# Small numbers of a fused encoder block in one tile, and where the matmuls' operands then start

## The chip, the core and the metric

The kernel runs on one core of a Trainium2 chip. A core has TensorE (PE; its weight loads are shown apart as PEld), VectorE (DVE), ScalarE (ACT), GpSimd (POOL) and SyncE (SP), which here issues the transfers. The metric is the time of one execution in device microseconds, the median of three runs. SBUF has 128 partitions; where a tile "starts" is the byte within each partition.

## The reference

One layer of an encoder block on 256 tokens of 2048 channels, all in float32:

```
u = rmsnorm(h) * g_mix;  proj = u @ w_in                 # 2048 x 4096
y_f = per group of 256 channels: Re(DFT2 over positions x channels) @ w_f[g]   # 4 groups
y_a = attention, 8 heads of 128, three dilated windows merged, ALiBi distances
h = h + concat(y_f, y_a) @ w_out                         # 2048 x 2048
u = rmsnorm(h) * g_mlp
h = h + square(relu(u @ w_up)) @ w_down                  # 2048 x 8192, 8192 x 2048
out = rmsnorm(h) * g_fin
```

## The kernel before

Every large product is made of three: a number is split into hi (as float32r, 12 significant bits) and lo (the rest), and hi*hi + hi*lo + lo*hi are added up in PSUM. Activations are split once into tiles that stay in SBUF (u, y_hi, y_lo). Weights are stored in the order of their use, in chunks of 128 partitions by 2048 numbers (1 MB). `load_next` brings a chunk into a w_raw buffer and splits it, in two halves, into w_hi (ACT, L112) and w_lo (DVE, L113); each of the three has three buffers, and two chunks are loaded ahead.

Two loops use the chunks:
- `strip` (matmuls of `mm3`, L120 to L122; the first chunk's at L197): the activations are stationary, the weights move. One strip is 4 chunks x 2 token tiles x 4 rows of tiles x 3 products = 96 matmuls of 512 columns.
- `column` (L220, L221): one chunk holds 128 columns of weights, which are stationary; the activations move. One column is 16 pairs: w_hi times u_hi and u_lo side by side (512 columns), then w_lo times u_hi (256 columns).

In time: two strips of w_in for the Fourier group, with the transforms' small products between them; twice a strip for v and eight columns for q and k, with the heads' attention between the groups; four strips of w_out; then four MLP groups, each of 16 columns (w_up) and four strips (w_down). Groups 0 and 2 keep their hidden activations in y tiles of the pool mlp, groups 1 and 3 in y tiles of the pool acts, which were the Fourier and attention groups' outputs before. The last strip is cut into parts (`products`), the last 72 matmuls having 256 columns, and the last norm (`ending`) follows.

The order of work on an engine is the order in which the program is written; small steps are put between the products by generators (`later`, `part`). Pools lay their tiles one behind the other, and each tile starts at a multiple of 32 bytes. The pool const holds ident and ones (512 bytes each) and root, one number a partition; wpool comes behind it, then acts, then four, att and mlp by turns in the same place. The norms' numbers (`inverse`, `sums`, `ending`) are tiles of acts of one to eight numbers a partition.

Of the kernel before, what the change touches and what calls it, by code (L numbers as in the profile page):

```python
# [16 lines left out]
P = 128  # L17
# [15 lines left out]
FIRST = (4, 4, 2, 2, 2)  # L33
WARM = 9


def _order():
    """The weights by chunks of 128 rows by 2048 numbers, in the order of their use.

    "rows": four row tiles by 512 columns, the moving operand; "cols": 16 row tiles by 128 columns,  # L40
    the stationary operand."""
    todo = []

    def rows(name, row0, col0):
        todo.extend((name, row0 + c * CK * P, CK, col0, NS) for c in range(NN))

    def cols(name, col0):
        todo.append((name, 0, KT, col0, P))

    rows("w_in", 0, 0)  # L50
    rows("w_in", 0, NS)
    for a in range(2):
        rows("w_in", 0, 3 * FOURIER + a * NS)
        for hd in range(a * 4, a * 4 + 4):
            cols("w_in", FOURIER + hd * HD)
            cols("w_in", 2 * FOURIER + hd * HD)
    for n in range(NN):
        rows("w_out", 0, n * NS)
    for gi in range(NGRP):
        for j in range(KT):  # L60
            cols("w_up", gi * D + j * P)
        for n in range(NN):
            rows("w_down", gi * D, n * NS)
    return todo
# [3 lines left out]
def tile_block(ctx: ExitStack, tc: tile.TileContext, gx_t, x, w_all, w_f, g_fin,  # L68
# [27 lines left out]
    nc.vector.memset(ones, 1.0)  # L96
    root = const.tile([P, 1], F32, name="root")
    nc.scalar.activation(root, ones[:, :1], AF.Sqrt)
# [3 lines left out]

    NG = 2 * KT
    gh = acts.tile([P, NG + NM * D], F32, name="gh")
    g_cols = gh[:, :NG]
# [3 lines left out]
    def split(hi, lo, src, scale=None):  # L109
        """hi + lo = src * scale, each in the 12 significant bits that one pass carries."""  # L110
        if scale is None:
            nc.scalar.copy(out=hi, in_=src)  # L112
            nc.vector.tensor_tensor(out=lo, in0=src, in1=f32(hi), op=ALU.subtract)  # L113
        else:
            nc.scalar.activation(hi, src, AF.Copy, scale=scale)
            nc.vector.scalar_tensor_tensor(out=lo, in0=src, scalar=scale, in1=f32(hi),
                                           op0=ALU.mult, op1=ALU.subtract)
# [5 lines left out]

# [1 line left out]
    def hidden_input():  # L125
        u = acts.tile([P, KT, 2 * S], F32R, name="u")
        return u, u[:, :, :S], u[:, :, S:]

    u, u_hi, u_lo = hidden_input()
    order = _order()  # L130
# [41 lines left out]
    def later(gen):  # L172
        """Work that a result asks for: its first part now, each further one after a group of the products that follow."""
        next(gen, None)
        queue.append(gen)
# [10 lines left out]
    def strip(l_hi, l_lo, need=None):  # L186
        """The activations (stationary) times 2048 rows by 512 columns of the weights, for both token tiles."""
        ps = [acc() for _ in range(NM)]
# [22 lines left out]
    def column(r, parts=(KT // 2 - 1, KT - 1), need=None):  # L211
        """128 columns of the weights (stationary), transposed, times the activations.

        The halves of the result, whose sum is asked for: the large products, and the small ones."""
        ps = acc()
        hi, lo = chunk()
        for kt in range(KT):
            if kt == need:
                finish()
            nc.tensor.matmul(ps, hi[:, kt, :], r[:, kt, :], start=kt == 0, stop=False)  # L220
            nc.tensor.matmul(ps[:, S:], lo[:, kt, :], r[:, kt, :S], start=False, stop=kt == KT - 1)  # L221
            if kt in parts:
                part()
        return ps[:, :S], ps[:, S:]
# [7 lines left out]
    def inverse(ss, name):  # L232
        """1 / sqrt(mean of squares + eps), from the sums of squares."""
        n = ss.shape[1]
        a = acts.tile([P, n], F32, name=f"{name}_a")
        nc.vector.tensor_scalar(out=a, in0=ss, scalar1=1.0 / D, scalar2=EPS, op0=ALU.mult, op1=ALU.add)
        r = acts.tile([P, n], F32, name=f"{name}_r")
        nc.scalar.activation(r, a, AF.Sqrt)
        y = acts.tile([P, n], F32, name=f"{name}_y")
        nc.vector.reciprocal(out=y, in_=r)  # L240
        t = acts.tile([P, n], F32, name=f"{name}_t")
        nc.vector.tensor_mul(out=t, in0=y, in1=y)
        nc.vector.tensor_mul(out=t, in0=t, in1=a)
        nc.vector.tensor_scalar(out=t, in0=t, scalar1=-0.5, scalar2=1.5, op0=ALU.mult, op1=ALU.add)
        inv = acts.tile([P, n], F32, name=f"{name}_inv")
        nc.vector.tensor_mul(out=inv, in0=y, in1=t)
        return inv

    def across(inv, room):
        """The tokens' numbers along the free axis, the same on all partitions (in PSUM)."""  # L250
        ps = aux()[:, :S]
        for m in range(NM):
            b = room()
            nc.vector.tensor_scalar_mul(out=b, in0=ones, scalar1=inv[:, m:m + 1])
            nc.tensor.transpose(ps[:, m * P:(m + 1) * P], b, ident)
        return ps

    y_hi = acts.tile([P, KT, S], F32R, name="y_hi")
    y_lo = acts.tile([P, KT, S], F32R, name="y_lo")

# [1 line left out]
    four_ctx = ExitStack()  # L262
# [23 lines left out]

    # cos(a + b) = cos a cos b - sin a sin b, on the even and odd parts along the channels.
    # The packed channels of group gl of two: 128 even ones, then 128 odd ones; the even channel 128,
    # apart, takes the place 32 * gl among the odd ones, and the odd one there the place 0.

    def fold_map(g):
        """The group's linear map after the transform along the channels."""
        wf_hi = four.tile([P, 2, GD], F32R, name="wf_hi")
# [12 lines left out]
    def symmetric(st, ps):  # L306
        """Even and odd parts along the channels."""
        e_hi = four.tile([P, NM, WU], F32R, name="e_hi")
# [25 lines left out]
    def positions(g):  # L334
        """The transform along the positions."""
        st, gl = divmod(g, 2)
# [23 lines left out]

# [1 line left out]
    inv_q = acts.tile([P, S], F32, name="inv_q")  # L362
    inv_k = acts.tile([P, S], F32, name="inv_k")
    inv1 = []
# [28 lines left out]

# [1 line left out]
    later(timeline({6: [(add_squares, 0), (add_squares, 4)]}))  # L395
# [19 lines left out]

# [1 line left out]
    att_ctx = ExitStack()  # L417
# [11 lines left out]
    def channels(ps, name, inv):  # L429
        """One head of q or k, with the head's channels on the partitions."""  # L430
        t = total(ps, att)
# [52 lines left out]

# [1 line left out]
    u2, u2_hi, u2_lo = hidden_input()  # L486
    junk = att.tile([P, NS], F32, name="junk")

# [3 lines left out]
    def sums(ss, name):  # L492
        t = acts.tile([P, ss.shape[1]], F32, name=f"{name}_s")
        nc.vector.tensor_reduce(out=t, in_=ss, op=ALU.add, axis=AX.X)
        return t

    ss2 = acts.tile([P, NM, NN], F32, name="ss2")

# [26 lines left out]

# [1 line left out]
    inv_u = acts.tile([P, S], F32, name="inv_k")  # L527
# [7 lines left out]

    ss3 = acts.tile([P, NM, NN], F32, name="ss3")
    for gi in range(NGRP):
# [22 lines left out]

# [1 line left out]
    NH2 = NS // 2  # L562
    tail = [[(acc(), slice(0, NS))], [(aux()[:, :NH2], slice(0, NH2)), (aux()[:, :NH2], slice(NH2, NS))]]
    base = acts.tile([P, NM], F32, name="base")
    got = []
# [14 lines left out]

    def small(name):
        return acts.tile([P, 1], F32, name=name)

    def ending(m):
        a = base[:, m:m + 1]
        for i, (ps, cols) in enumerate(tail[m]):
            hs = h[m][:, D - NS + cols.start:D - NS + cols.stop]
            nc.vector.tensor_add(out=hs, in0=hs, in1=ps)
            b = small(f"a{m}{i}")
            nc.vector.tensor_tensor_reduce(out=junk[:, cols], in0=hs, in1=hs, scale=1.0 / D, scalar=a,  # L590
                                           op0=ALU.mult, op1=ALU.add, accum_out=b)
            a = b
        r, y, t, inv = (small(f"{n}{m}") for n in ("r", "y", "t", "i"))
        nc.scalar.activation(r, a, AF.Sqrt)
# [54 lines left out]
def _tiles(weights):  # L649
    """All weights in one array, a chunk after the other, each with its partitions' numbers in a row."""  # L650
    todo = _order()
# [32 lines left out]
```

## Time and profile before

| | |
|---|---|
| time, median of 3 runs | 1036.84 us (1036.69 to 1037.19) |
| profiled execution, first to last instruction | 1035.5 us |
| time of that execution beyond its span | not recorded; the median lies 1.3 us above the span |
| PE, DVE, ACT busy | 99%, 59%, 49% of the span |
| transfers' share of 16 engines | 53.5% |
| matmuls of 512 columns | 3536 |
| matmuls of 256 columns | 1628 |

How to read it: a matmul's own time in the trace is longer than the distance to the next one, since matmuls overlap; its end is modelled. The starts of two neighbours show the rate. In "acc<-u,w_hi" the first operand moves and the second is stationary.

### The profile page before, as it was taken

The numbers are of one execution on the slowest core, as the hardware profiler recorded it, in microseconds if no ns is written. First come the engines' busy times: TensorE is split into PE (matmuls) and PEld (weight loads), VectorE is DVE, ScalarE is ACT, GpSimd is POOL, SyncE is SP. The second block draws the span as 40 slices with busy tenths as digits, with TensorE's granted clock in tenths as the row PEclk, the third lists the DMA queues.
The fourth block names the chain that finished last, engine by engine and source line by source line (L and its number), as shares of the span: only waits on it lengthen the run. The fifth ranks groups of instructions, "written<-read, shape, count | busy, mean of one in ns | idle before, by whom it ended". The sixth has DMA issues, their size and how long they took to land.

```text
span 1035.5 us, 12994 instructions
## 1 busy us (share of the span) xinstructions
PE 1026.0 (99%) x5254; PEld 870.2 (84%) x5254; DVE 610.2 (59%) x846; ACT 502.4 (49%) x741; POOL 1.3 (0%) x10
## 2 busy tenths in 40 slices
PE   9999999999999999999999999999999999999997
PEld 7888888888888888888888888888888888888886
DVE  6875775775456656545656545456555446565553
ACT  7754554554446554333555533345543335554441
POOL 0000000000000000000000000000000000000000
PEclk9999999999999999999999999999999999999999
DMA  9653755444555555555555555555555555555532
GB/s 320 229 223 112 265 170 189 164 170 163 187 220 172 194 191 180 198 202 177 191 194 174 201 186 180 203 172 194 192 180 197 202 178 189 192 177 200 183 142 82
DMA packets 32683, 195.10 MB, mean 188 GB/s; under 512 B 3568, under 2 KB 6128, under 8 KB 10608
## 3 DMA queue, kind: packets, MB, share of 16 engines
q1 hardware_dynamic: 32624, 194.28, 53.5%
q8 instruction: 41, 0.67, 0.2%
q14 instruction: 18, 0.15, 0.0%
HBM read 192.17 MB, written 2.10 MB: 188 GB/s over the span
## 4 chain that ended last, share of the span: by engine, by line
PE 97%; DMA 1%; SPq 0%; DVE 0%; ACT 0%; issue 0%; ACTq 0%
PE acc L220 29%; PE acc L122 16%; PE acc L120 16%; PE acc L121 16%; PE acc L221 15%; PE aux L122 1%; PE aux L120 1%; PE aux L121 1%; DMA w_raw<-w_all 1%; SPq L91 0%; PE aux L509 0%; PE aux L464 0%; DVE w_lo L113 0%; ACT w_hi L112 0%; ACT gh L607 0%
## 5 line engine op out<-in xcount | busy, mean ns | idle before, releaser
L113 DVE TENSOR_TENSOR w_lo<-w_raw,w_hi 128x1024 fp32r<-128x1024 f32 (+1 forms) x356 | 423.8, 1209 | 286.5 <-ACT w_hi L112 286.2
L112 ACT CAST w_hi<-w_raw 128x1024 fp32r<-128x1024 f32 (+1 forms) x356 | 361.8, 1040 | 319.4 <-PE acc L122 230.5
L220 PE MATMUL acc<-u,w_hi 128*128 128x512 f32 x1280 | 450.9, 394 | 0.0
L221 PE MATMUL acc<-u,w_lo 128*128 128x256 f32 x1280 | 362.0, 283 | 0.0
L220 PEld LDWEIGHTS acc<-u,w_hi 128*128 128x128 f32 x1280 | 240.4, 188 | 54.7
L120 PE MATMUL acc<-w_hi,y_hi 128*128 128x512 f32 x624 | 246.7, 395 | 0.0
L122 PE MATMUL acc<-w_hi,y_lo 128*128 128x512 f32 x624 | 245.6, 394 | 0.0
L121 PE MATMUL acc<-w_lo,y_hi 128*128 128x512 f32 x624 | 244.5, 392 | 0.0
L221 PEld LDWEIGHTS acc<-u,w_lo 128*128 128x128 f32 x1280 | 240.7, 188 | 0.2
L122 PEld LDWEIGHTS acc<-w_hi,y_lo 128*128 128x128 f32 x624 | 117.3, 188 | 27.5
L121 PEld LDWEIGHTS acc<-w_lo,y_hi 128*128 128x128 f32 x624 | 117.4, 188 | 26.3
L120 PEld LDWEIGHTS acc<-w_hi,y_hi 128*128 128x128 f32 x624 | 117.4, 188 | 25.4
L533 ACT ACTIVATE sq<-relu 128x256 f32<-128x256 f32 x64 | 26.8, 419 | 118.7 <-DVE relu L531 118.7
L113 DVE TENSOR_TENSOR y_lo<-sq,y_hi 128x256 fp32r<-128x256 f32 x64 | 27.2, 425 | 58.1 <-ACT y_hi L112 58.1
L121 PE MATMUL acc<-w_lo,u 128*128 128x512 f32 x120 | 47.6, 397 | 0.5 <-DVE w_lo L113 0.5
L122 PE MATMUL acc<-w_hi,u 128*128 128x512 f32 x120 | 47.4, 395 | 0.0
L120 PE MATMUL acc<-w_hi,u 128*128 128x512 f32 x120 | 46.9, 398 | 0.1
L229 DVE TENSOR_TENSOR total<-acc,total 128x256 f32<-128x256 f32 x80 | 33.5, 418 | 2.7 <-ACT total L228 2.6
L228 ACT COPY total<-acc 128x256 f32<-128x256 f32 x80 | 29.2, 366 | 8.1 <-PE acc L221 8.1
L556 DVE TENSOR_TENSOR gh<-gh,acc 128x512 f32<-128x512 f32 x30 | 20.5, 684 | 17.9 <-PE acc L122 17.8
L121 PEld LDWEIGHTS acc<-w_lo,u 128*128 128x128 f32 x120 | 22.6, 188 | 5.9 <-DVE w_lo L113 1.4
L112 ACT CAST y_hi<-sq 128x256 fp32r<-128x256 f32 x64 | 26.0, 406 | 2.0
(142 smaller groups left out, 472.5 us busy)
## 6 DMA issues: line engine op xcount, KB each, us to landing
w_raw<-w_all SPq DMA_DIRECT2D x171, 1024.0 KB, 4.7
w_raw<-w_all SPq DMA_DIRECT2D x6, 512.0 KB, 7.7
w_raw<-w_all SPq DMA_DIRECT2D x8, 256.0 KB, 5.0
gh<-x SPq DMA_DIRECT2D x8, 256.0 KB, 7.0
out<-gh SPq DMA_DIRECT2D x6, 256.0 KB, 2.4
gh<-gx_t SPq DMA_DIRECT2D x4, 256.0 KB, 6.3
wf<-w_f SPq DMA_DIRECT2D x4, 256.0 KB, 4.9
g_b<-g_fin SPq DMA_DIRECT2D x1, 1024.0 KB, 4.7
```

Source lines behind the costliest of these rows:

```text
L112: nc.scalar.copy(out=hi, in_=src)
L113: nc.vector.tensor_tensor(out=lo, in0=src, in1=f32(hi), op=ALU.subtract)
L120: nc.tensor.matmul(ps, l_hi, r_hi, start=first, stop=False)
L121: nc.tensor.matmul(ps, l_hi, r_lo, start=False, stop=False)
L122: nc.tensor.matmul(ps, l_lo, r_hi, start=False, stop=last)
L220: nc.tensor.matmul(ps, hi[:, kt, :], r[:, kt, :], start=kt == 0, stop=False)
L221: nc.tensor.matmul(ps[:, S:], lo[:, kt, :], r[:, kt, :S], start=False, stop=kt == KT - 1)
L228: nc.scalar.copy(out=t, in_=ps[1])
L229: nc.vector.tensor_tensor(out=t, in0=ps[0], in1=t, op=ALU.add)
L533: nc.scalar.activation(q, r, AF.Square)
L556: nc.vector.tensor_add(out=hs, in0=hs, in1=ps[m])
```

## The change

A tile few of 224 numbers a partition (896 bytes) joins the pool const, and a function `small` hands out slices of it one behind the other. The norms' numbers, ss2, ss3, base and those of `ending` become such slices. The pool acts is filled in another order: u, y_hi, y_lo, inv_q and inv_k come ahead of gh (which holds 32 gains and then the residual h). Comments and docstrings go; no instruction is added, removed or moved on any engine, and none has another wait. Core of the diff:

```
-    root = const.tile([P, 1], F32, name="root")
+    few = const.tile([P, FEW], F32, name="few")          # FEW = 224
+    few_at = [0]
+    def small(n, *shape):
+        at = few_at[0]
+        few_at[0] += n
+        assert few_at[0] <= FEW
+        t = few[:, at:at + n]
+        return t.rearrange("p (a b) -> p a b", b=shape[0]) if shape else t
+    root = small(1)
...
     NG = 2 * KT
+    u0 = acts.tile([P, KT, 2 * S], F32R, name="u")
+    y_hi = acts.tile([P, KT, S], F32R, name="y_hi")
+    y_lo = acts.tile([P, KT, S], F32R, name="y_lo")
+    inv_q = acts.tile([P, S], F32, name="inv_q")
+    inv_k = acts.tile([P, S], F32, name="inv_k")
     gh = acts.tile([P, NG + NM * D], F32, name="gh")
...
-        a = acts.tile([P, n], F32, name=f"{name}_a")
+        a = small(n)
...
-    ss2 = acts.tile([P, NM, NN], F32, name="ss2")
+    ss2 = small(NM * NN, NN)
...
-    base = acts.tile([P, NM], F32, name="base")
+    base = small(NM)
...
-        r, y, t, inv = (small(f"{n}{m}") for n in ("r", "y", "t", "i"))
+        r, y, t, inv = (small(1) for _ in range(4))
```

Where the tiles start, by the addresses in the two programs (byte in the partition, with its rest by 64 and by 2048):

| tile | before | after |
|---|---|---|
| ident, ones | 16512, 17024 (0; 128, 640) | the same |
| first w_raw; each further w_raw, w_hi, w_lo buffer 8192 on | 17568 (32; 1184) | 18432 (0; 0) |
| u | 107808 (32; 1312) | 92160 (0; 0) |
| y_hi, y_lo of acts | 140576, 156960 (32; 1312) | 124928, 141312 (0; 0) |
| y_hi, y_lo of mlp | 186464, 202848 (32; 96) | 186496, 202880 (0; 128) |
| h in gh | 91424 (32; 1312) | 159872 (0; 128) |
| tables, maps, q, k, v, p of four and att | all (32; several) | all (0; several) |

All slices that a matmul takes of these tiles start at multiples of 512 bytes from the tile's start.

## Rows read from the trace of the kernel before

**Rows 1.** The page, part 1: span, busy time of each engine.
```profile
span 1035.5 us, 12994 instructions
PE 1026.0 (99%) x5254; PEld 870.2 (84%) x5254; DVE 610.2 (59%) x846; ACT 502.4 (49%) x741; POOL 1.3 (0%) x10
```

**Rows 2.** Waits of PE: us in total, times, longest.
```profile
PE aux L101 <- DVE ones L96: 1.1, 1, 1.1
PE acc L121 <- DVE w_lo L113: 0.5, 1, 0.5
```

**Rows 3.** The page, part 4: the chain that ended last, by engine.
```profile
PE 97%; DMA 1%; SPq 0%; DVE 0%; ACT 0%; issue 0%; ACTq 0%
```

**Rows 4.** The page, part 2: granted TensorE clock in 40 slices.
```profile
PEclk9999999999999999999999999999999999999999
```

**Rows 5.** Groups by line and shape, PE and PEld: count | busy us, mean ns.
```profile
L220 PE MATMUL acc<-u,w_hi 128*128 128x512 f32 x1280 | 450.9, 394 | 0.0
L221 PE MATMUL acc<-u,w_lo 128*128 128x256 f32 x1280 | 362.0, 283 | 0.0
L120 PE MATMUL acc<-w_hi,y_hi 128*128 128x512 f32 x624 | 246.7, 395 | 0.0
...
L120 PE MATMUL acc<-w_hi,u 128*128 128x512 f32 x120 | 46.9, 398 | 0.1
L122 PE MATMUL aux<-w_hi,y_lo 128*128 128x256 f32 x32 | 9.0, 282 | 0.0
...
L464 PE MATMUL aux<-ident,s 128*128 128x128 f32 x32 | 4.8, 272 | 0.0
...
L120 PE MATMUL aux<-wf_hi,tab_hi 128*128 128x256 f32 x16 | 4.7, 292 | 0.0
...
L220 PEld LDWEIGHTS acc<-u,w_hi 128*128 128x128 f32 x1280 | 240.4, 188 | 54.7
```

**Rows 6.** Timeline of PE at four stage boundaries: start us, us, instruction.
```profile
403.47 0.39 PE L120 MATMUL acc<-w_hi,y_hi 128*128 128x512 f32 x1
...
491.37 0.40 PE L220 MATMUL acc<-u,w_hi 128*128 128x512 f32 x1
...
581.25 0.40 PE L120 MATMUL acc<-w_hi,y_hi 128*128 128x512 f32 x1
...
670.47 0.40 PE L220 MATMUL acc<-u,w_hi 128*128 128x512 f32 x1
```

**Rows 7.** Timeline of PE, the first and last of the closing 256-column matmuls.
```profile
1019.12 0.28 PE L120 MATMUL aux<-w_hi,y_hi 128*128 128x256 f32 x1
...
1027.55 0.28 PE L122 MATMUL aux<-w_hi,y_lo 128*128 128x256 f32 x1
```

**Rows 8.** Timeline of PE, four transposes in one head.
```profile
119.46 0.60 PE L464 MATMUL aux<-ident,s 128*128 128x128 f32 x4
```

**Rows 9.** Timeline behind the last matmul, two of the small instructions.
```profile
1029.29 0.22 DVE L596 SCALAR_TENSOR_TENSOR t<-y,a 128x1 f32<-128x1 f32 x1
1029.54 0.15 DVE L597 TENSOR_SCALAR t<-t 128x1 f32<-128x1 f32 x1
```

**Rows 10.** Two windows: length, busy us (x) of PE, PEld, DVE, ACT, POOL; clock; transfers.
```profile
5.25:18.71 13.46, 12.77 (x50) 9.02 (x51) 10.17 (x19) 10.22 (x20) 0.00 (x0) 1.00 0.99 333
18.71:1027.83 1009.12, 1009.12 (x5186) 857.31 (x5186) 596.46 (x816) 487.94 (x715) 0.58 (x4) 1.00 0.53 187
```

**Rows 11.** The chain in order of time, 4 to 20 us: start, us.
```profile
10.85 5.47 DMA w_raw<-w_all
...
18.71 0.51 PE acc L121
```

**Rows 12.** Waits of ACT for PE: us in total, times, longest.
```profile
ACT w_hi L112 <- PE acc L122: 230.5, 73, 4.5
...
ACT w_hi L112 <- PE acc L220: 71.3, 74, 3.5
```

**Rows 13.** The page, part 6: transfers of whole chunks, median us to landing.
```profile
w_raw<-w_all SPq DMA_DIRECT2D x171, 1024.0 KB, 4.7
```

**Rows 14.** Timeline of PE in group 1's strips: the longest distance there.
```profile
641.20 0.40 PE L120 MATMUL acc<-w_hi,y_hi 128*128 128x512 f32 x1
641.44 0.40 PE L121 MATMUL acc<-w_lo,y_hi 128*128 128x512 f32 x1
```

More of the change, by code (lines that the diff above doesn't have):

```diff
@@ L34 @@
 WARM = 9
+FEW = 224
 def _order():
@@ L122, in mm3, with hidden_input @@
         nc.tensor.matmul(ps, l_lo, r_hi, start=False, stop=last)
-    def hidden_input():
-        u = acts.tile([P, KT, 2 * S], F32R, name="u")
+    def hidden_input(u):
         return u, u[:, :, :S], u[:, :, S:]
-    u, u_hi, u_lo = hidden_input()
+    u, u_hi, u_lo = hidden_input(u0)
     order = _order()
@@ L234, in inverse @@
         n = ss.shape[1]
-        a = acts.tile([P, n], F32, name=f"{name}_a")
+        a = small(n)
         nc.vector.tensor_scalar(out=a, in0=ss, scalar1=1.0 / D, scalar2=EPS, op0=ALU.mult, op1=ALU.add)
-        r = acts.tile([P, n], F32, name=f"{name}_r")
+        r = small(n)
         nc.scalar.activation(r, a, AF.Sqrt)
-        y = acts.tile([P, n], F32, name=f"{name}_y")
+        y = small(n)
         nc.vector.reciprocal(out=y, in_=r)
-        t = acts.tile([P, n], F32, name=f"{name}_t")
+        t = small(n)
         nc.vector.tensor_mul(out=t, in0=y, in1=y)
@@ L244, in inverse @@
         nc.vector.tensor_scalar(out=t, in0=t, scalar1=-0.5, scalar2=1.5, op0=ALU.mult, op1=ALU.add)
-        inv = acts.tile([P, n], F32, name=f"{name}_inv")
+        inv = small(n)
         nc.vector.tensor_mul(out=inv, in0=y, in1=t)
@@ L256, in across @@
         return ps
-    y_hi = acts.tile([P, KT, S], F32R, name="y_hi")
-    y_lo = acts.tile([P, KT, S], F32R, name="y_lo")
     four_ctx = ExitStack()
@@ L359, in mapped @@
         split(y_hi[:, 2 * g:2 * g + 2, :], y_lo[:, 2 * g:2 * g + 2, :], py)
-    inv_q = acts.tile([P, S], F32, name="inv_q")
-    inv_k = acts.tile([P, S], F32, name="inv_k")
     inv1 = []
@@ L483, in tile_block @@
             later(head(hd, q, k, v, (2, 3, 2) if hd < NH - 1 else (2, 3, 1)))
-    u2, u2_hi, u2_lo = hidden_input()
+    u2, u2_hi, u2_lo = hidden_input(acts.tile([P, KT, 2 * S], F32R, name="u"))
     junk = att.tile([P, NS], F32, name="junk")
@@ L492, in sums @@
     def sums(ss, name):
-        t = acts.tile([P, ss.shape[1]], F32, name=f"{name}_s")
+        t = small(ss.shape[1])
         nc.vector.tensor_reduce(out=t, in_=ss, op=ALU.add, axis=AX.X)
         return t
-    ss2 = acts.tile([P, NM, NN], F32, name="ss2")
+    ss2 = small(NM * NN, NN)
     def residual(ps, n):
@@ L534, in up @@
         split(hidden[0][:, j, :], hidden[1][:, j, :], q)
-    ss3 = acts.tile([P, NM, NN], F32, name="ss3")
+    ss3 = small(NM * NN, NN)
     for gi in range(NGRP):
@@ L579, in products @@
                 kt == 0, kt == KT - 1)
-    def small(name):
-        return acts.tile([P, 1], F32, name=name)
     def ending(m):
@@ L588, in ending @@
             nc.vector.tensor_add(out=hs, in0=hs, in1=ps)
-            b = small(f"a{m}{i}")
+            b = small(1)
             nc.vector.tensor_tensor_reduce(out=junk[:, cols], in0=hs, in1=hs, scale=1.0 / D, scalar=a,
```

## The prediction

> **What bounds the kernel now.** I read the share of each engine first, then who TensorE waits for, then the chain of work that ended last. TensorE (PE) has a matmul in flight for 1026.0 of 1035.5 us, VectorE (DVE) works 59% and ScalarE (ACT) 49% [rows 1]. PE's own waits come to 1.6 us in two places [rows 2], and the chain is 97% PE [rows 3]. So the time is the number of matmuls times the distance between the starts of two neighbours, and the change can move the time by much only if it moves that distance. No other engine and no transfer need be faster for it.
>
> "Busy" does not say that PE runs at its peak. The granted clock is 9 (full) in every slice [rows 4], that is 2.4 GHz, so 512 columns should stream in 512 / 2.4 = 213.3 ns and 256 in 106.7 ns. The mean of one matmul (394 ns, 283 ns) [rows 5] overlaps with the next and is no price; the distance of starts is. It comes out of stage boundaries, since the code gives the number of matmuls between them [rows 6]:
> - strips of MLP group 0 (403.47 to 491.37 us, 4 strips of 96 matmuls of 512 columns): 87.90 us / 384 = 228.9 ns
> - strips of group 1 (581.25 to 670.47): 89.22 / 384 = 232.3 ns
> - columns of group 1 (491.37 to 581.25, 16 columns of 16 pairs, 512 + 256): 89.88 / 256 = 351.1 ns a pair, where 320.0 would do
> - the 72 last matmuls of 256 columns (1019.12 to 1027.55, 71 distances) [rows 7]: 118.7 ns.
>
> A fixed cost per matmul can be had from the transposes: four take 0.60 us together [rows 8], the last alone 0.272 [rows 5], so they start 0.109 us apart. That reads as 256 steps at 2.4 GHz (106.7 ns) and 2.6 ns over. Their moving operand is ident; with ones it is the only operand of a matmul that starts at a multiple of 64 bytes before the change. Every other one, the stationary ones of the transposes included, starts 32 bytes past one.
>
> Taking 2.6 ns off, the excess over streaming is 13.0 ns in group 0's strips: 31 steps in 512 columns, about one in 16 columns, which are 64 bytes of a partition. I call this term A: 13.3 ns for 512 columns, 6.7 for 256. With A out, 3.1 ns (7 steps) are left in group 1's strips, 2.7 in the last matmuls of 256 columns, and 25.9 - 20.0 = 5.9 for two in the columns; next to none in group 0's strips. This is term B, some 3 ns a matmul. Group 0 and group 1 run the same lines on the same weights' buffers and differ in where the stationary tile lies (pool mlp, 96 past a multiple of 2048; pool acts, 1312 past). So one part of the distance does hang on where operands lie.
>
> **The change part by part.** Both programs hold the same instructions in the same order on every engine, with the same waits; only tile names and addresses differ.
>
> *The shared tile.* The square root, the inverses and the last norm's numbers become slices of few. Nothing is added or removed. On the path that sets the end stand only those behind the last matmul, seven or so instructions of 0.15 to 0.22 us [rows 9]. If a slice 4 bytes past the last one made each a tenth faster or slower, that would be under 0.2 us; I take 0, since these instructions read one or two numbers either way.
>
> *The products' operands.* All large tiles move from 32 bytes past a multiple of 64 to a multiple of 64; w_raw, w_hi, w_lo, u and the y of pool acts to a multiple of 2048, the y of pool mlp to 128 past one. I take term A for the price of starting in the middle of 64 bytes and take it away: one step in 16 columns is what each 64 bytes, read in two halves, would cost, and the aligned moving operand of the transposes shows no A. The trace has no matmul of 32-bit numbers at full column rate on an aligned moving operand, so the term is bounded and not read: from below by 0 (the distance stays), from above by all the excess over 2.6 ns.
> Counts [rows 5]: 512 columns 1280 + 3 x 624 + 3 x 120 = 3512 (the three lines of mm3 have one count each; the 24 first ones are left out); 256 columns 1280 + 3 x 32 + 15 x 16 = 1616. Before 18.71 us, 50 matmuls stand [rows 10] behind the first transfers and splits, and the chain there is not PE's [rows 11]; 26 of them are among the 3512 and gain nothing. Sum: 3486 x 13.33 = 46.5 us, 1616 x 6.67 = 10.8 us, together 57.3 us.
>
> *What is late next.* Nothing, by these rows. ACT's splits of weights wait 230.5 + 71.3 us for PE [rows 12], so they come earlier when PE does. From 18.71 us on DVE works 596 and ACT 488 of 1009 us [rows 10]; on a span shorter by 57 us that is 63% and 51%. A chunk of weights takes PE 24 x 232.3 ns = 5.6 us now and 5.3 us then, against 4.7 us to land with three buffers [rows 13]. Where DVE is busiest, at the start (10.2 of 13.5 us in the first stretch of the same group), this cover is thinnest; were it gone there, a few us of the gain would go.
>
> *Sum.* The profiled span is 1035.5 us, the median of the runs 1036.84, so 1.3 us lie around the span. 1035.5 - 57.3 + 1.3 = 979.5, say 980 us. If B went too, everything would run at its columns and 2.6 ns: 768 x 13.0 (groups 0 and 2) + 1280 x 25.9 (pairs) + 1438 x 16.4 + 336 x 9.4 ns = 10.0 + 33.2 + 23.6 + 3.2 = 70.0 us, and 967. The forecast's own range is 965 to 990.
>
> The Trainium skill, page "TensorE: Matmul & The Clock Gate", section Back-to-back issue gap, gives N / 2.4 + 2.5 ns for an isolated warm matmul, 215.8 for 512 columns. The distances above differ from it by 13 to 17 ns, the transposes agree with its 2.5 by 2.6; where it held everywhere the estimate would be the 967 just worked out from rows.
>
> **The rivals.**
> *No change: the excess belongs to reading four bytes a column.* The transposes have half the rate of columns, so they may have room to hide what A is. Then A stays, B at most shifts a little, and the time stays 1036.8. For it: A is the same in places with quite different addresses mod 2048. Against it: the difference of groups 0 and 1 shows that place matters.
> The Trainium skill, page "SBUF — State Buffer", section Specifications, has lines of 16 bytes, and a penalty where an access crosses to a new one. 32 past a multiple of 64 starts such a line as well as 0 does, so by it this change is worth nothing and the time is 1036.8. The trace speaks for 64 and not 16 bytes, with one step in 16 columns, but it does not show the cause.
>
> *Half: only the ends of an operand cost.* 2048 bytes that start in the middle touch 33 blocks of 64 for 32, 1024 bytes 17 for 16. One block of 16 columns is 6.7 ns a matmul, whatever its columns: (3486 + 1616) x 6.67 = 34.0 us, so 1003. Against it: the excess grows with the columns, from 9.4 to 16.4 ns.
>
> *Slower: the two operands collide more.* Stationary and moving operand are read at the same time, a weight load of 188 ns [rows 5] within each 229 or 232. Now they lie 128 (group 1) or 64 bytes (group 0) apart modulo 512. After it, weights, u and y all start at the same place modulo 2048, and group 0's pair has the 128 of group 1 now. If B is such a collision, group 0 and 2's 768 matmuls take group 1's distance, 3.4 ns more: 2.6 us, 1039.4. If equal starts are the worst place, each 512 takes what the worst in the steady strips takes today, 0.24 us [rows 14]: 768 x 11.1 + 2744 x 7.7 = 29.6 us, 1066. It decides from the point where B's growth is above what A gives back, that is with A untouched and the strips over 0.232. For it: B exists and hangs on place. Against it: B is only a fifth of A.
>
> **How the numbers follow.** Forecast (A goes) 0.48, 980; half 0.18, 1003; no change 0.14, 1036.8; slower 0.20, 1039 to 1066. The likeliest is 980. A range from 962 to 1040 holds the first three and the lowest part of the fourth, some 8 in 10. Faster by over 0.2% (2.1 us, about what a measurement of this kernel can tell from no change): 0.48 + 0.18 = 0.66; within: 0.14; slower: 0.20.
>
> **What would show it.** Right: starts in the strips 0.216 to 0.219 us apart and 0.325 to 0.331 a pair in the columns; the transposes still 0.109, weight loads still about 188 ns, PE still 97% of the chain, instructions of DVE and ACT as long as before. Half: 0.222 to 0.226. No change: 0.229 and 0.232 in the same stages. Slower: group 0's strips at or over group 1's. What would make it wrong with A gone: waits of PE for w_hi or w_lo of more than a few us in total, at the start above all.

## The result, and the profile after

The changed kernel takes 1031.67 us (median of 5 runs, 1031.38 to 1032.38) against 1036.84 us before: a ratio of 0.9948, 95% interval 0.9936 to 0.9961. It is faster, by 5.2 us. The forecast was 980 us: the direction was right, the size was wrong by a factor of eleven, and the time lies inside the range only because the range reached to the other cases.

The page of the changed kernel, parts 1 and 4:

```profile
span 1030.6 us, 12994 instructions
PE 1021.0 (99%) x5254; PEld 868.8 (84%) x5254; DVE 609.7 (59%) x846; ACT 502.7 (49%) x741; POOL 1.3 (0%) x10
...
PE 97%; DMA 1%; SPq 0%; DVE 0%; ACT 0%; issue 0%; ACTq 0%
```

Against [rows 1, 3] PE's time fell by 5.0 us and the span by 4.9, weight loads by 1.4, and DVE and ACT changed by at most 0.5: the gain is in the matmuls, as the prediction argued it must be. Its timeline at the stage boundaries, as in [rows 6] (start us, us, instruction; here from the last boundary ahead of w_out's strips on):

```profile
216.71 0.40 PE L138 MATMUL acc<-w_hi,y_hi 128*128 128x512 f32 x1
...
309.91 0.39 PE L237 MATMUL acc<-u,w_hi 128*128 128x512 f32 x1
...
399.88 0.39 PE L138 MATMUL acc<-w_hi,y_hi 128*128 128x512 f32 x1
...
489.11 0.39 PE L237 MATMUL acc<-u,w_hi 128*128 128x512 f32 x1
...
579.55 0.40 PE L138 MATMUL acc<-w_hi,y_hi 128*128 128x512 f32 x1
...
666.62 0.39 PE L237 MATMUL acc<-u,w_hi 128*128 128x512 f32 x1
...
757.06 0.39 PE L138 MATMUL acc<-w_hi,y_hi 128*128 128x512 f32 x1
...
846.30 0.39 PE L237 MATMUL acc<-u,w_hi 128*128 128x512 f32 x1
...
935.05 0.39 PE L138 MATMUL acc<-w_hi,y_hi 128*128 128x512 f32 x1
```

The boundaries before that [rows 6] leaves out:

```profile
217.44 0.39 PE L120 MATMUL acc<-w_hi,y_hi 128*128 128x512 f32 x1
...
312.51 0.40 PE L220 MATMUL acc<-u,w_hi 128*128 128x512 f32 x1
...
760.34 0.40 PE L120 MATMUL acc<-w_hi,y_hi 128*128 128x512 f32 x1
...
848.25 0.40 PE L220 MATMUL acc<-u,w_hi 128*128 128x512 f32 x1
...
938.14 0.40 PE L120 MATMUL acc<-w_hi,y_hi 128*128 128x512 f32 x1
```

Differences of these starts give the length of each stage. Strips have 384 matmuls, columns 256 pairs:

| stage | before, us | after, us | ns a matmul or pair, before | after |
|---|---|---|---|---|
| strips of w_out | 95.07 | 93.20 | | |
| columns, group 0 | 90.96 | 89.97 | | |
| strips, group 0 | 87.90 | 89.23 | 228.9 | 232.4 |
| columns, group 1 | 89.88 | 90.44 | 351.1 | 353.3 |
| strips, group 1 | 89.22 | 87.07 | 232.3 | 226.7 |
| columns, group 2 | 89.87 | 90.44 | 351.1 | 353.3 |
| strips, group 2 | 87.91 | 89.24 | 228.9 | 232.4 |
| columns, group 3 | 89.89 | 88.75 | 351.1 | 346.7 |

(The w_out stage and the columns of group 0 hold the transposes and a wait for the second norm too.) The strips of w_out and of group 1 got faster, and so did those of w_in and of group 3, which the table leaves out; the strips of groups 0 and 2 got slower and took the very pace that group 1 had before. The columns split into a faster pace (346.7) and a slower one (353.3). No stage came near 216 to 219 ns. The transposes' row shows that their distance stayed, at (0.60 - 0.272) / 3 = 0.109 us as in [rows 8]:

```profile
118.87 0.60 PE L476 MATMUL aux<-ident,s 128*128 128x128 f32 x4
```

The 72 last matmuls of 256 columns run from 1014.15 to 1022.67 us, 8.52 / 71 = 120.0 ns; [rows 7] gave 118.7, so these got slower.

### The profile page after: what moved, and what is told of

Same layout as the page of the kernel before. It is cut to its first block, busy times and chain, and to the rows that moved or that the text cites. A ratio compares the mean times of both kernels' runs of the same rounds, so it can differ in the third digit from the quotient of the medians.

```text
span 1030.6 us, 12994 instructions
## 1 busy us (share of the span) xinstructions
PE 1021.0 (99%) x5254; PEld 868.8 (84%) x5254; DVE 609.7 (59%) x846; ACT 502.7 (49%) x741; POOL 1.3 (0%) x10
## 4 chain that ended last, share of the span: by engine, by line
PE 97%; DMA 1%; SPq 0%; DVE 0%; ACT 0%; issue 0%; ACTq 0%
PE acc L237 29%; PE acc L139 16%; PE acc L140 16%; PE acc L138 16%; PE acc L238 15%; PE aux L138 1%; PE aux L140 1%; PE aux L139 1%; DMA w_raw<-w_all 1%; SPq L92 0%; PE aux L521 0%; PE aux L476 0%; DVE w_lo L131 0%; ACT w_hi L130 0%; ACT gh L616 0%
## 5 line engine op out<-in xcount | busy, mean ns | idle before, releaser
L543 DVE SCALAR_TENSOR_TENSOR relu<-total,inv_k 128x256 f32<-128x256 f32 x64 | 26.8, 419 | 0.0
```

The source lines that it names most:

```text
L543: nc.vector.scalar_tensor_tensor(out=r, in0=total(ps, mlp), scalar=0.0, in1=inv_u, op0=ALU.max, op1=ALU.mult)
```

## The experiments

The theories at the start: (1) the distance of starts hangs on the place of the stationary operand relative to the moving one, and the rest by 64 is nothing; (2) a start in the middle of 64 bytes costs, as the prediction had it; (3) what is over 213.3 ns is the weight load beside the matmul, or the four bytes a column.

**Everything 32 bytes further (shift_32).**

```
-FEW = 224
+FEW = 232
```

> The changed kernel with the shared tile 32 bytes longer, so that every large tile starts 32 bytes past a multiple of 64 and all places relative to each other stay. Theory 1 (relative place): as the changed kernel, 1031.7 us, strips of groups 1 and 3 at 226.7 ns, of groups 0 and 2 at 232.4. Theory 2 (the rest by 64): the gain is lost, 1036.8 us or more.

It took 1031.77 us (ratio 0.9953, 0.9941 to 0.9966): nothing of the gain is lost. Its timeline at the boundaries of groups 0 and 1:

```profile
399.19 0.39 PE L138 MATMUL acc<-w_hi,y_hi 128*128 128x512 f32 x1
...
488.42 0.39 PE L237 MATMUL acc<-u,w_hi 128*128 128x512 f32 x1
...
578.86 0.40 PE L138 MATMUL acc<-w_hi,y_hi 128*128 128x512 f32 x1
...
665.93 0.39 PE L237 MATMUL acc<-u,w_hi 128*128 128x512 f32 x1
```

89.23, 90.44 and 87.07 us: each stage as long as in the changed kernel. Theory 2 is out.

**The old order of tiles on the new start (old_order).**

```
+    gh = acts.tile([P, NG + NM * D], F32, name="gh")
     u0 = acts.tile([P, KT, 2 * S], F32R, name="u")
...
     inv_k = acts.tile([P, S], F32, name="inv_k")
-    gh = acts.tile([P, NG + NM * D], F32, name="gh")
```

> The changed kernel with gh ahead of u and y again, as before the change: all large tiles stay at multiples of 64 bytes, but u and all y lie 128 bytes past the weights modulo 512. Theory 1 (relative place): every strip at 232.4 ns, so before's time plus 768 x 3.4 ns = 1039.4 us, slower than before. Theory 2 (the rest by 64): no slower than the changed kernel, 1031.7 us.

It took 1039.44 us, slower than before (ratio 1.0026, 1.0016 to 1.0035), though every large tile starts at a multiple of 64 bytes. The strips of groups 0 and 1:

```profile
403.53 0.40 PE L138 MATMUL acc<-w_hi,y_hi 128*128 128x512 f32 x1
...
492.75 0.40 PE L237 MATMUL acc<-u,w_hi 128*128 128x512 f32 x1
...
582.63 0.40 PE L138 MATMUL acc<-w_hi,y_hi 128*128 128x512 f32 x1
...
671.85 0.40 PE L237 MATMUL acc<-u,w_hi 128*128 128x512 f32 x1
```

Both are 89.22 us, 232.3 ns: group 1 as before the change, group 0 at its pace. The shared tile by itself is a loss of 2.6 us, since it moves the y of groups 0 and 2 from 448 to 128 bytes past the weights modulo 512; the gain came from laying u and y ahead of gh.

**A map of places (map_places).** One moving tile mv, one stationary tile st, and runs such as

```
for r in range(0, 512, 32):
    run(0, r)        # 48 matmuls, mv from byte 0, st from byte r on
run(32, 32)
run(32, 160)
run(16, 16)
...
```

> This kernel leaves out the whole block; it holds only runs of 48 matmuls (128 x 512, both operands float32r) on one moving and one stationary tile, a transpose ahead of each run as a mark, and writes one product as output. Between the runs only the stationary tile's start changes, in steps of 32 bytes, against the moving one's. Theory 1 (the distance of starts hangs on the place of the stationary operand relative to the moving one, modulo 512 bytes, and not on the rest by 64): about 226.7 ns a matmul at 0, 232.4 at 128, 229.0 at 448, other values between; the runs with both operands 32 bytes past a multiple of 64 like those with both at one (226.7 for equal places, 232.4 for 128 apart). Theory 2 (a start in the middle of 64 bytes costs): the runs at odd multiples of 32 are slower by several ns than their neighbours, and 32 with 32 is slower than 0 with 0. Theory 3 (what is left over 213.3 ns comes from the weight load that runs beside the matmul): with 64 or 32 stationary columns the distance falls towards 216 ns; if it belongs to reading four bytes a column it stays at 226 to 232, and falls to 216 for bfloat16 alone.

Rows of its timeline, one for each run (start, length of the 48 matmuls):

```profile
31.43 11.16 PE L62 MATMUL acc<-mv,st 128*128 128x512 f32 x48
...
42.46 11.44 PE L62 MATMUL acc<-mv,st 128*128 128x512 f32 x48
...
53.76 11.45 PE L62 MATMUL acc<-mv,st 128*128 128x512 f32 x48
...
76.42 11.39 PE L62 MATMUL acc<-mv,st 128*128 128x512 f32 x48
...
98.98 11.23 PE L62 MATMUL acc<-mv,st 128*128 128x512 f32 x48
...
121.37 11.16 PE L62 MATMUL acc<-mv,st 128*128 128x512 f32 x48
...
188.95 11.23 PE L62 MATMUL acc<-mv,st 128*128 128x512 f32 x48
...
211.34 11.16 PE L62 MATMUL acc<-mv,st 128*128 128x512 f32 x48
...
222.37 11.44 PE L62 MATMUL acc<-mv,st 128*128 128x512 f32 x48
...
233.67 11.45 PE L62 MATMUL acc<-mv,st 128*128 128x512 f32 x48
...
244.98 11.72 PE L62 MATMUL acc<-mv,st 128*128 128x512 f32 x48
...
279.14 11.30 PE L62 MATMUL acc<-mv,st 128*64 128x512 f32 x48
...
290.30 11.34 PE L62 MATMUL acc<-mv,st 128*64 128x512 f32 x48
...
301.50 11.35 PE L62 MATMUL acc<-mv,st 128*32 128x512 f32 x48
...
312.73 11.33 PE L62 MATMUL acc<-mv,st 128*32 128x512 f32 x48
...
324.00 10.52 PE L62 MATMUL acc<-mvb,stb 128*128 128x512 bf16 x48
...
334.47 10.52 PE L62 MATMUL acc<-mvb,stb 128*128 128x512 bf16 x48
```

They are, in order, the places 0, 32, 64, 128, 192, 256 and 448; then both operands 32 past a multiple of 64 at equal places, the same 128 apart, both 16 past and both 4 past at equal places; 64 stationary columns at the places 0 and 128, 32 columns at 0 and 128; bfloat16 at 0 and 128. A row is the first distance behind the mark (0.31 to 0.32 us), 46 further ones and the last matmul (0.39). So place 0 has (11.16 - 0.39 - 0.31) / 46 = 227 ns, 32 and 64 have 233, 128 has 232, 192 and 448 have 229, and 256 is as 0; the slowest of the sixteen, 96, has 234. Every one of the eight places from 256 on agrees within 0.2 ns with the place 256 bytes ahead of it: for 512 columns the map repeats after 256 bytes.

Both operands 32 past a multiple of 64 at equal places are again 227: theory 1, a second time. With 128 bytes between them they have 233.3, a nanosecond more than the 232.4 expected, a small miss that stays open. Relative place is not all, though: with both 16 past it is 233 and with both 4 past 239, in spite of equal places, so the rule holds for starts at multiples of 32.

Weight loads of 64 and 32 columns leave the distance at 230 to 231, so the excess over 213.3 ns is not the load's length. But they take the place away: 0 and 128 bytes differ by 5 ns with 128 stationary columns and by 1 ns or less with 64 or 32. bfloat16, without a longer first distance, has (10.52 - 0.38) / 47 = 215.7 ns at both places: it has only 2.4 ns over 213.3, float32r 13 to 21 at starts that are multiples of 32. The excess and its hanging on place thus go with float32r; that it is the four bytes a column and not the format itself is not shown.

The map's runs of 256 columns, timed in the same way, have 119.7 ns at place 0, 120.0 at 128, 118.7 at 384 and 117.8 at 448. There equal places are not the best, and 128 and 384 differ, so the period of 256 bytes is not shown for them.

The Trainium skill, page "SBUF — State Buffer", section Specifications (TRN2), speaks of lines of 16 bytes; by that alone 16 past would be as good as 32 past, and here it costs 6 ns, so the measurement decides. The Trainium skill, page "TensorE: Matmul & The Clock Gate", section Back-to-back issue gap, has N / 2.4 + 2.5 ns, 215.8, for an isolated matmul; the bfloat16 run, a steady stream, agrees with it (215.7), the float32r runs do not.

**Groups 0 and 2 at equal places too (mlp_at_0).**

```
     mlp = ctx.enter_context(tc.tile_pool(name="mlp", bufs=1))
+    mlp.tile([P, 96], F32, name="pad")
```

> The changed kernel with 384 unused bytes at the head of the pool mlp, so that the y tiles of groups 0 and 2 start at a multiple of 512 like the weights. Theory 1 (relative place): their strips go from 232.4 to 226.7 ns, 768 x 5.7 ns = 4.4 us less: 1027.3 us. Theory 2 (the rest by 64): no change, 1031.7 us.

It took 1030.49 us (ratio 0.9937, 0.9923 to 0.9951), 1.2 us less than the changed kernel and not 4.4. Its timeline at the boundaries of group 0, and of group 3's columns:

```profile
309.54 0.39 PE L237 MATMUL acc<-u,w_hi 128*128 128x512 f32 x1
...
401.06 0.40 PE L138 MATMUL acc<-w_hi,y_hi 128*128 128x512 f32 x1
...
488.10 0.39 PE L237 MATMUL acc<-u,w_hi 128*128 128x512 f32 x1
...
843.12 0.39 PE L237 MATMUL acc<-u,w_hi 128*128 128x512 f32 x1
...
933.56 0.40 PE L138 MATMUL acc<-w_hi,y_hi 128*128 128x512 f32 x1
```

Group 0's strips fell to 87.04 us, as expected, and so did group 2's. But the columns of group 0 went from 89.97 to 91.52 us, where no operand of a matmul had moved; those of group 3 went from 88.75 to 90.44. That took 3.2 us back.

**Two paces at one place (entry_paces).** Runs of 32 pairs at equal places, with 0 to 7 short matmuls ahead:

```
for j in range(8):
    before(j)        # a transpose, then j matmuls of 256 columns
    ps = pairs(0, 0, count=32)
```

> This kernel leaves out the whole block, as map_places does. 32 pairs (512 + 256 columns) with equal places, eight times, each behind a transpose and 0 to 7 matmuls of 256 columns; the same with 384 bytes between the operands, six times; then 40 matmuls of 512 columns with equal places and with 128 bytes, six times each. Theory 1a (two paces, chosen by the moment of entry): the pairs with equal places come out at 346.7 or 353.3 ns with the count ahead of them, the runs with equal places always at 226.7 to 227, those at 128 at 232.4 or 233.4. If entry does not matter, each place has one pace.

The third and last 512-column matmul of the run with none ahead, then the first and last of the run with one ahead (its columns as in the timelines above):

```profile
32.38 0.39 PE L69 MATMUL acc<-mv,st 128*128 128x512 f32 x1
...
42.43 0.39 PE L69 MATMUL acc<-mv,st 128*128 128x512 f32 x1
...
43.01 0.39 PE L69 MATMUL acc<-mv,st 128*128 128x512 f32 x1
...
53.95 0.40 PE L69 MATMUL acc<-mv,st 128*128 128x512 f32 x1
```

10.05 / 29 = 346.6 ns a pair, and 10.94 / 31 = 352.9. Of the eight runs, those behind 0, 2 and 4 short matmuls settled at 346.7, the other five at 353.0 to 353.4, and kept it to their end. The paces are patterns: in the fast one every pair is alike (230 and 117 ns), in the slow one pairs of about 350, 361 and 349 ns take turns. The six runs with 384 bytes between the operands all settled at 351.0 to 351.3, the pace of the columns before the change. The runs of like matmuls at equal places settled at 226.7 each time; those at 128 bytes at 232.4.

So at equal places a stream of pairs has two paces, and what ran ahead can decide between them, with the same addresses. That this is how group 3's columns came out fast and those of groups 1 and 2 slow fits, but it isn't shown what decides there: groups 1 and 3 of the changed kernel are entered behind strips of the same lines at the same places, and one settled slow, the other fast. It isn't one buffer of PSUM either, since the 16 columns of a stage take the acc buffers by turns and keep one pace.

**Columns in runs of like matmuls (grouped, grouped_before).**

```
+        if need is None:
+            for kt in range(KT):
+                tc.keep_in_program_order(
+                    nc.tensor.matmul(ps, hi[:, kt, :], r[:, kt, :], start=kt == 0, stop=False))
+                if kt == 11:
+                    part()
+            for kt in range(KT):
+                tc.keep_in_program_order(
+                    nc.tensor.matmul(ps[:, S:], lo[:, kt, :], r[:, kt, :S], start=False, stop=kt == KT - 1))
+            part()
+            return ps[:, :S], ps[:, S:]
```

> The kernel of mlp_at_0 with the columns' products in another order: all 16 of 512 columns, then all 16 of 256, in place of pairs (the one column that waits for the last rows of u keeps its pairs). Theory 1a (the place sets the rate of a run of like matmuls; in pairs the engine falls into one of two paces, 346.7 or 353.3 ns a pair, and it was the slow one in all groups of mlp_at_0): like matmuls take 226.7 and 119.8 ns whatever came before, 346.5 a pair; four column stages of 88.7 in place of 90.4 to 91.5 us and the 16 columns of q and k 0.9 us less a half: 1030.5 - 8.7 = 1021.8 us. Theory 4 (pairs or runs are the same; the stages of 88.75 us were chance of the entry): 1027 to 1031 us.

> The kernel before the change, with the columns' products grouped as in the run above and no address moved. Weights and u lie 128 bytes apart modulo 512 there. Theory 1a: runs at that place take 232.4 (or 233.4) and 118.7 ns, 351.1 to 352.1 a pair, as the pairs do now: 1036.8 to 1038 us, no gain. Theory 4b (grouping helps by itself, since w_lo is wanted later or a pair's short matmul costs more): faster than 1036.8 by several us.

On mlp_at_0 it took 1026.40 us (1025.47 to 1026.80; ratio to before 0.9896, 0.9880 to 0.9911), the fastest version here and 5.3 us ahead of the changed kernel. It was to be 1021.8. Its boundaries:

```profile
308.32 0.39 PE L248 MATMUL acc<-u,w_hi 128*128 128x512 f32 x1
...
400.55 0.40 PE L138 MATMUL acc<-w_hi,y_hi 128*128 128x512 f32 x1
...
487.62 0.39 PE L237 MATMUL acc<-u,w_hi 128*128 128x512 f32 x1
...
576.66 0.40 PE L138 MATMUL acc<-w_hi,y_hi 128*128 128x512 f32 x1
```

The columns of group 1 take 89.04 us for 90.44, of which 88.7 was expected: after each change from 256 to 512 columns five distances of 229 to 236 ns come ahead of the 227. The columns of group 0 lost instead, 92.23 for 91.52, and PE's waits (us in total, times, longest) have a new one there. L283 is a transpose of the second norm's numbers; the trace names nothing that released it:

```profile
PE aux L283 <- issue: 1.8, 1, 1.8
```

On the kernel before, the same order took 1039.21 us, slower than before (ratio 1.0022, 1.0013 to 1.0030), where I had expected 1036.8 to 1038: the columns of group 1 are

```profile
493.02 0.40 PE L220 MATMUL acc<-u,w_hi 128*128 128x512 f32 x1
...
582.98 0.39 PE L120 MATMUL acc<-w_hi,y_hi 128*128 128x512 f32 x1
```

89.96 us against 89.88, and the rest is group 0's wait, 1.8 us there too. So the order gains only where the places are equal, and there only against the slow pace: group 3's columns in the changed kernel, in pairs at the fast pace, took 88.75 us.

## Why the prediction was wrong

- What bounds the kernel: right. The time moved with the distance of starts and nothing else, and of the four distances that were read three, 228.9, 232.3 and 351.1, came out again at the same relative places (448, 128 and 384) in runs that hold nothing but matmuls. The fourth, 118.7 ns at 128 bytes, was 120.0 there.
- The step that failed is the price of the products' operands: "I take term A for the price of starting in the middle of 64 bytes and take it away", 57.3 us. It is worth 0: shift_32 puts every large tile back to 32 past a multiple of 64 and keeps the whole gain. One step in 16 columns looked like a block of 64 bytes, but it was a coincidence of one pace; at equal places the excess is 226.7 - 213.3 - 2.6 = 10.8 ns, 26 steps and not 32. The excess is there at every place with float32r and is gone with bfloat16 (215.7), as the rival called no change had it, which laid it to four bytes a column. That rival had the price of alignment right, but not the time (1036.8), since the places relative to each other moved as well.
- The evidence for term A was weak where it mattered: the transposes were the one aligned operand, but also ran at half the rate of columns. The prediction named this and still gave A about half the chance.
- Place, the prediction's term B, was the whole effect. B was read rightly as some 3 ns that hang on place, but the forecast left it as it was. That the time fell, as forecast, is luck: it fell by the term that was to stay. The rival "slower" was about B, and its first step was exact: groups 0 and 2 took group 1's distance, 2.6 us, and the stages lost 1.33 + 1.32. Its second step was wrong in sign: for 512 columns equal places are the best and not the worst, 226.7 for 232.3. Strips of w_out and groups 1 and 3 with w_in's gained some 7.1 us (1.9 for w_out, 2.2 for group 1), all columns 0.6 on balance, and the strips of groups 0 and 2 gave 2.6 back. The columns' 0.6 is luck of the entry as well: in mlp_at_0, with all four MLP groups at the slow pace, all columns together take some 2.6 us more than before the change.
- Half (1003): out with A, since it too was a price for the rest by 64.
- The edit's own cost of 0: right within what shows; from the end of the last matmul to the end of the span are 7.7 us before and after. The 1.3 us around the span compare the median with another execution's span; of one and the same execution they are 1.8 (1032.38 against 1030.6), which changes nothing here.
- What is late next: nothing, as stated; PE's waits are 1.8 us in total, after 1.6.

Shown: for matmuls of 512 columns at starts that are multiples of 32, the relative place sets the pace, with a period of 256 bytes; the rest by 64 does not; the excess goes with float32r. Open: whether it is its four bytes a column, and of which operand; why the place counts for 5 ns with 128 stationary columns and hardly with 64; what makes 256 bytes; what picks one of the two paces of pairs at equal places. No place gave float32r less than 226.7 ns for 512 columns.

## What to carry to other kernels

Where a kernel is a stream of float32r matmuls, measure the distance of starts by stage, and compare stages that differ only in which tile is stationary: 1.5% between them said more than any rule on alignment. For runs of 512 columns lay stationary and moving tiles at equal places modulo 256 bytes, at a multiple of 32; where lengths alternate, equal places can also lose (353.3 ns a pair for 351.1), so time it. Test by shifting everything at once and one tile alone, which tells alignment from relative place. A price fitted to a number that looks like a round block is a guess until one operand has been moved.

## What the runs showed of the hardware

Two operands of a matmul influence each other by their addresses, though nothing waits on a semaphore: 226.7 to 234 ns for 512 columns at starts that are multiples of 32, without any change in instructions. The Trainium skill, page "TensorE: Matmul & The Clock Gate", section Step-by-step: what each phase is for, says that loading the next weights does not steal read bandwidth from the running matmul; the map of places does not fit that for float32r. There the place of the stationary operand moves the distance by up to 7 ns, and by 1 ns when the load has 64 columns. The granted clock is full in every slice of the changed kernel's page as in [rows 4]. A steady stream can hold one of two paces for a whole stage of 90 us, so a small edit far away can move the time by 1.7 us a stage: group 0's columns took 89.97 and 91.52 us with the same addresses.
